# Norm statistics of the first unit by halves of 256 positions, and a new order of the first stage

## The chip, the core and the metric

The kernel runs on one core of one Trainium2 chip. The metric is the device time of one execution in microseconds (us). Five engines of the core work side by side, each through its own list of instructions in order: TensorE (PE in the profile, with PEld for its weight loads), VectorE (DVE), ScalarE (ACT), GpSimd (POOL) and SyncE (SP, which here only issues DMAs). An instruction waits on semaphores until its inputs are there; whatever is listed behind it on the same engine waits with it.

## The reference

One layer: a norm with modulation, an input projection into four parts, a Fourier branch and a recurrent branch with gates, an output projection, a residual and a last norm. What matters here is the head of it:

```python
def rmsnorm(x, g):
    xf = x.astype(jnp.float32)
    y = xf * lax.rsqrt(jnp.mean(xf * xf, axis=-1, keepdims=True) + EPS)
    return (y * g.astype(jnp.float32)).astype(x.dtype)

def modulate(x, g, shift, scale):
    return rmsnorm(x, g) * (1.0 + scale) + shift
...
mod = jax.nn.silu(c) @ w_ada[l] + b_ada[l]
shift, scale, gate = jnp.split(mod[:, None, :], 3, axis=-1)
hx = modulate(x, norm_gain[l], shift, scale)          # x: (1, 2048, 1024)
uf_x, gf_x, ul_x, gl_x = in_proj(hx, w_in[l])         # hx @ w_in, split in four parts of 512
yl_x, _, _ = lru_branch(ul_x, ...)
yf_x = fourier_branch(uf_x, w_four[l])
x = x + gate * out_proj(yf_x, gf_x, yl_x, gl_x, w_out[l])
return rmsnorm(x, final_gain)
```

## The kernel before

The 2048 positions are worked in four units of 512, and the 256 context positions are a fifth. In the first stage a unit's x lies transposed in SBUF: 128 of the 1024 features on the partitions (a k-tile, eight of them), 512 positions along the free dimension. The tiles `xt` hold two k-tiles each. Three multiplications per k-tile and unit go to TensorE:

- `pul` (`mms_ul`, L328): the normalised slice times the weights of the recurrent branch, twelve matmuls of 512 columns; each product is made of three, with operands split in a high and a low part (`hl` and `wu`).
- `ptt` (`mms_tt`, L343): sums and differences of the slice (`f`, split into `eo`) times weights of the Fourier branch (`wf`), twelve matmuls of 260 or 252 columns.
- In the first unit alone also the making of those operands: `part` (`ada_part`, L128) and `o` (`ada_sum`, L143) compute shift and scale of the k-tile from `blk` blocks of w_ada, which `ada_fin` turns into `sh` and `gn`; `pw` (`four_mm`, L168) makes the Fourier weights from `wr`, a slice of w_in.

The first unit has to have its norm statistics before any of this. Its squares `sq` (`square0`, L199) are summed over k-tiles on VectorE (`sum0`, L207); `col0` (L211) sums over partitions by a matmul with ones, four matmuls (eight passes in the profile, since a float32 product takes two) into `ss`; `stats` (L225) takes the root on ScalarE and the reciprocal on VectorE; `spread` (L248) turns that into `pr`, a row per position on all partitions; `prep_x` (L272) multiplies x by it, `prep_hi` (L279) applies `gn` and `sh` and writes the high part of `hl`, `prep_lo` (L312) the low part. Warm-up matmuls (`warm`, L460) on a tile of ones stand ahead.

The order is a list written out by hand, `S1` (L43). Each word is a letter for one of the functions above (`ops`, L477) and its numbers; the program issues them in that order, and each engine gets its own share of them in it. `X` loads x, `a` a half of a w_ada block, `w` a slice of w_in, `0` and `9` small constants; `1`, `+`, `3` are squares, sums and column sums, `T` the root and reciprocal, `P` the spread; `A b c d` make shift and scale, `i j J` the Fourier weights, `u U` the weights of the recurrent branch; `x h l` normalise and split a k-tile, `f e o` fold it; `m` is `pul`, `t` is `ptt`, `!` warm-up, `r` a copy of `pr` into SBUF (`rb`). `x0.1` is unit 0, k-tile 1.

All loads named here are issued by SP in that order on one hardware queue, and `vecs`, a table of small vectors, by ScalarE's queue at the start. SP issues a DMA only when the eighth DMA before it on these queues has landed.

For k-tile 0 `pul` has an order of its own, so that it can begin with the high parts:

```python
if u == 0 and k == 0:
    for s, t in ((0, 0), (1, 0), (0, 1)):
        for c in range(c0, c1):
            nc.tensor.matmul(pul[u][c], w[:, s, P * c:P * c + P], hl[:, t], start=s + t == 0, stop=False)
    return
```

Of the kernel before, what the change touches and what calls it, by code (L numbers as in the profile page):

```python
# [55 lines left out]
def tile_layer(ctx, tc, xp, xnat, xt_in, ctxn, ctxt, w_ada, vec, bgate, fgain, w_in, w_g, w_four, w_gate, w_out,  # L56
# [13 lines left out]
    def r(ap):  # L70
        return ap.bitcast(F32)
# [200 lines left out]
    def prep_x(u, k):  # L272
        n = 256 if u == "c" else 512
        x = xts[u, k // 2][:, k % 2, 0:n]
        nc.vector.tensor_tensor(out=x, in0=x, in1=rb[u][:, 0:n], op=ALU.mult)
# [3 lines left out]
    def prep_hi(u, k):  # L279
        which = 1 if u == "c" else 0  # L280
        n = 256 if u == "c" else 512
        x = xts[u, k // 2][:, k % 2, 0:n]
        h = hs[u, k] = p1.tile([P, 512], F32, name=f"h{u}_{k}", tag="h", bufs=4)
        hl = slab[u, k] = p1.tile([P, 2, 512], F32R, name=f"hl{u}_{k}", tag="hl", bufs=4)
        g, b = gn[:, k, which:which + 1], sh[:, k, which:which + 1]
        if u == 0 and k == 0:
# [1038 lines left out]
```

## Time and profile before

| | us |
|---|---|
| median of 3 runs (653.13 to 653.5) | 653.2 |
| profiled execution, its own time | 653.59 |
| span of its instructions | 651.8 |
| TensorE busy in the span | 642.2 |
| VectorE busy | 524.7 |
| ScalarE busy | 423.9 |
| first `pul` matmul starts at | 16.47 |
| first `ptt` matmul starts at | 22.00 |

Times inside the execution count from the start of the span. In the rows further down a timeline row reads: start, duration, engine, line, operation, out<-in, shapes, count, and in brackets how long the engine had been idle and what released it. TensorE's durations overlap, since matmuls are pipelined: the distance from one start to the next tells what a matmul costs, and the chain of waits shows these distances summed. A granted clock of 1.00 is the upper of TensorE's two levels, 2.4 GHz; the other is 1.2 GHz.

### The profile page before, as it was taken

To read this page: it belongs to the slowest core of one execution; us is meant where nothing else is said; L and a number is where in the kernel's file an instruction comes from. 1 tells how busy PE (TensorE), PEld (TensorE's weight loads), DVE (VectorE), ACT (ScalarE), POOL (GpSimd) and SP (SyncE) were. 2 spreads that over 40 slices of the span, in tenths; PEclk is the share of its full clock that TensorE was granted. 3 is DMA by queue.
4 is the path that set the end of the run, shared out by engine and by line. 5 is a ranking of instruction groups with operands and counts; after the bars stand their busy time and mean duration, and the time that the engine had idled before them with its cause. 6 is when DMAs were issued, how large, how long until landed. Compare 5 with 4: busy or idle time off the path is not lost.

```text
span 651.8 us, 10756 instructions
## 1 busy us (share of the span) xinstructions
PE 642.2 (99%) x4076; PEld 564.9 (87%) x4076; DVE 524.7 (80%) x853; ACT 423.9 (65%) x612; POOL 105.7 (16%) x170
## 2 busy tenths in 40 slices
PE   8999999999999999999999999999999999999996
PEld 8788888888988889899998999999988888888885
DVE  4767999877767668578989898897989697998886
ACT  5575777557554455669597695977844667753752
POOL 0100101023031123442221212212210000000000
PEclk9999999999999999999999999999999999999999
DMA  8996886629597694535443434432477887327533
GB/s 332 417 381 231 244 286 171 246 82 279 151 310 255 236 324 132 166 106 165 129 153 110 145 108 165 123 122 81 145 251 231 290 278 263 107 98 247 184 117 130
DMA packets 69886, 130.22 MB, mean 200 GB/s; under 512 B 7076, under 2 KB 39972, under 8 KB 69834
## 3 DMA queue, kind: packets, MB, share of 16 engines
q1 hardware_dynamic: 51066, 82.36, 39.3%
q0 software_dynamic: 12384, 39.00, 17.8%
q10 hardware_dynamic: 6384, 8.18, 4.0%
q8 instruction: 32, 0.52, 0.3%
q14 instruction: 20, 0.16, 0.1%
HBM read 91.24 MB, written 38.27 MB: 199 GB/s over the span
## 4 chain that ended last, share of the span: by engine, by line
PE 91%; DVE 4%; DMA 2%; issue 2%; ACT 1%; POOL 0%; DVEq 0%; ACTq 0%; POOLq 0%
PE pg L74 9%; PE pg L76 9%; PE pg L75 9%; PE po L75 9%; PE po L76 9%; PE po L74 9%; PE pul L74 5%; PE pul L76 4%; PE pul L75 4%; PE ptt L74 2%; PE ptt L75 2%; PE ptt L76 2%; PE pl L74 2%; PE pl L75 2%; PE pl L76 2%
## 5 line engine op out<-in xcount | busy, mean ns | idle before, releaser
L74 PE MATMUL pg<-hg,wg 128*128 128x256 f32 x512 | 144.1, 282 | 0.1
L75 PE MATMUL pg<-hg,wg 128*128 128x256 f32 x512 | 143.6, 280 | 0.4 <-DVE hg L711 0.4
L76 PE MATMUL pg<-hg,wg 128*128 128x256 f32 x512 | 143.8, 281 | 0.0
L74 PEld LDWEIGHTS pg<-hg,wg 128*128 128x128 f32 x512 | 96.3, 188 | 2.9 <-issue 1.3
L75 PEld LDWEIGHTS pg<-hg,wg 128*128 128x128 f32 x512 | 96.3, 188 | 1.4 <-DVE hg L711 0.7
L76 PEld LDWEIGHTS pg<-hg,wg 128*128 128x128 f32 x512 | 96.4, 188 | 0.0
L427 POOL DMA_DIRECT2D g_d<-gs x80 | 57.8, 724 | 151.9 <-DVE gs L761 72.6
L75 PE MATMUL po<-wo,y 128*128 128x512 f32 x160 | 63.1, 394 | 0.0
L76 PE MATMUL po<-wo,y 128*128 128x512 f32 x160 | 63.1, 394 | 0.0
L74 PE MATMUL po<-wo,y 128*128 128x512 f32 x160 | 62.9, 393 | 0.0
L74 PE MATMUL pul<-hl,wu 128*128 128x512 f32 x124 | 49.9, 402 | 0.0
L76 PE MATMUL pul<-hl,wu 128*128 128x512 f32 x124 | 48.9, 395 | 0.0
L75 PE MATMUL pul<-hl,wu 128*128 128x512 f32 x124 | 48.8, 394 | 0.0
L855 ACT ACTIVATE g<-pl,vecs 128x1024 f32<-128x1024 f32 x32 | 35.4, 1117 | 13.5 <-PE pl L76 13.5
L290 ACT ACTIVATE h<-xt,sh,gn 128x512 f32<-128x512 f32 x31 | 25.2, 813 | 20.4 <-DVE gn L152 10.4
L811 DVE SCALAR_TENSOR_TENSOR v<-up,vecs,v 128x1284 f32<-128x1284 f32 (+1 forms) x24 | 34.1, 1419 | 3.9 <-ACT v L804 3.2
L74 PE MATMUL ptt<-wf,eo 128*128 128x260 f32 (+1 forms) x128 | 36.5, 285 | 0.0
L74 PEld LDWEIGHTS po<-wo,y 128*128 128x128 f32 x160 | 30.3, 189 | 7.1
L76 PE MATMUL ptt<-wf,eo 128*128 128x260 f32 (+1 forms) x128 | 36.2, 283 | 0.0
L75 PE MATMUL ptt<-wf,eo 128*128 128x260 f32 (+1 forms) x128 | 36.2, 283 | 0.0
L76 PEld LDWEIGHTS po<-wo,y 128*128 128x128 f32 x160 | 30.0, 188 | 7.0
L75 PEld LDWEIGHTS po<-wo,y 128*128 128x128 f32 x160 | 30.0, 188 | 6.9
(330 smaller groups left out, 1669.2 us busy)
## 6 DMA issues: line engine op xcount, KB each, us to landing
xt<-in_xt_dram SPq DMA_DIRECT2D x16, 512.0 KB, 5.7
blk<-in_w_ada_dram SPq DMA_DIRECT2D x16, 512.0 KB, 9.4
hr<-h_d SPq DMA_DIRECT2D x32, 256.0 KB, 4.2
xr<-in_xnat_dram SPq DMA_DIRECT2D x16, 512.0 KB, 3.8
g<-g_d SPq DMA_DIRECT2D x15, 512.0 KB, 7.2
out_dram<-xr POOLq DMA_DIRECT2D x14, 512.0 KB, 3.3
dm<-in_dct_dram POOLq DMA_DIRECT2D x12, 514.0 KB, 8.5
x<-in_xp_dram SPq DMA_DIRECT2D x12, 512.0 KB, 5.7
```

Of the source, the lines that this page charges most:

```text
L74: nc.tensor.matmul(out_, lh, rh, start=first, stop=False, skip_group_check=skip)
L75: nc.tensor.matmul(out_, lh, rl, start=False, stop=False, skip_group_check=skip)
L76: nc.tensor.matmul(out_, ll, rh, start=False, stop=last, skip_group_check=skip)
L290: nc.scalar.activation(out=h[:, 0:n], in_=x, func=AF.Identity, scale=g, bias=b)
L427: queue.dma_start(dst[:, :, row:row + s1 - s0], s[:, :, P * i - off + s0:P * i - off + s1])
L811: nc.vector.scalar_tensor_tensor(out=v[:, 0:w], in0=up[:, j:j + w], scalar=cw[:, j:j + 1], in1=v[:, 0:w], op0=ALU.mult, op1=ALU.add)
L855: nc.scalar.activation(out=t[:, c0:c0 + cn], in_=pg[:, 0:cn], func=AF.Sigmoid, bias=vecs[:, q:q + 1])
```

## The change

The statistics of the first unit are made in two halves of 256 positions. Its x comes in another layout, so that a load (`X0.q.hf`) brings one half of the positions of two k-tiles, 256 KB in place of 512 KB; there are eight such loads in place of four, and the second four stand behind the first w_ada block, the first slice of w_in and the small constants. A square now covers two k-tiles of one half (eight squares, all on ScalarE; before seven there and one on VectorE). Of each four squares three are summed on VectorE, so there are two sums per half; two column sums per half (four in all, before three); root, reciprocal and spread run once per half. For k-tile 0 `x`, `h`, `l` and `pul` run by halves: 24 matmuls of 256 columns in place of 12 of 512. All other k-tiles and units are computed as before, in part from strided views of the same tiles.

`S1` is written anew. Its head, up to the first Fourier group `t0.0`, and the diff of the functions:

```diff
-S1 = "X0.0 X0.1 X0.2 X0.3 9 a0.0 a0.1 w0 0 70 !21 10 11 +1 12 13 +2 +3 2 14 15 +5 16 17 4 +7 w1 30 a1.0 a1.1 a2.0 !1 31 !1 32 A0 T0 P0 b0 x0.0 c0 d0 u0 h0.0 U0 a2.1 l0.0 f0.0 i0 e0.0 s0.0 r o0.0 j0 w2 m0.0.0 i1 j1 J0 a3.0 J1 A1 u1 b1 4 w3 m0.0.2 U1 c1 d1 x0.1 h0.1 f0.1 e0.1 t0.0
+S1 = "X0.0.0 X0.1.0 X0.2.0 X0.3.0 9 a0.0 a0.1 w0 0 X0.0.1 2 X0.1.1 X0.2.1 X0.3.1 70 !15 10 11 +1 12 +2 30 13 w1 31 A0 4 a1.0 T0.0 a1.1 a2.0 P0.0 b0 !1 u0 x0.0.0 c0 d0 h0.0.0 U0 l0.0.0 14 15 +5 i0 j0 16 +6 m0.0.0.0 m0.0.2.0 17 32 33 T0.1 P0.1 J0 x0.0.1 A1 b1 h0.0.1 l0.0.1 w2 i1 m0.0.0.1 m0.0.2.1 j1 a3.0 J1 u1 f0.0 e0.0 s0.0 r o0.0 w3 4 U1 a2.1 c1 d1 x0.1 h0.1 f0.1 e0.1 t0.0
...
     def square0(k):
-        x = xts[0, k // 2][:, k % 2, :]
...
-        if k == 7:
-            nc.vector.tensor_tensor(out=sq, in0=x, in1=x, op=ALU.mult)
-        else:
-            nc.scalar.activation(out=sq, in_=x, func=AF.Square)
+        x = xts[0, k % 4][:, k // 4, :]
...
+        nc.scalar.activation(out=sq, in_=x, func=AF.Square)
     def sum0(k):
-        acc = sts["sq", 0 if k < 4 else k - 1]
+        acc = sts["sq", 4 * (k // 4)]
...
     def col0(j):
...
-        acc = sts["sq", (0, 4, 6)[j]]
+        acc = sts["sq", (0, 3, 4, 7)[j]]
         for i in range(4):
-            nc.tensor.matmul(sts["ss"][:, 64 * i:64 * i + 64], acc[:, P * i:P * i + P], ones[:, 0:64],
-                             start=j + i == 0, stop=j == 2, skip_group_check=True)
+            c0 = 128 * (j // 2) + 64 * (i % 2)
+            nc.tensor.matmul(sts["ss"][:, c0:c0 + 64], acc[:, P * i:P * i + P], ones[:, 0:64],
+                             start=j + i == 0, stop=j == 3, skip_group_check=True)
...
-    def stats(u):
+    def stats(u, hf=0):
...
+            nc.scalar.activation(out=st[:, 4 + 2 * hf:6 + 2 * hf], in_=sts["ss"][:, 128 * hf:128 * hf + 128:64],
+                                 func=AF.Sqrt, scale=1.0 / D, bias=eps_t)
+            nc.vector.reciprocal(out=st[:, 2 * hf:2 * hf + 2], in_=st[:, 4 + 2 * hf:6 + 2 * hf])
...
-    def mms_ul(u, k, c0=0, c1=4):
+    def mms_ul(u, k, c0=0, c1=4, hf=None):
...
-        if u == 0 and k == 0:
+        if hf is not None:
+            p0 = 256 * hf
             for s, t in ((0, 0), (1, 0), (0, 1)):
                 for c in range(c0, c1):
-                    nc.tensor.matmul(pul[u][c], w[:, s, P * c:P * c + P], hl[:, t], start=s + t == 0, stop=False)
+                    nc.tensor.matmul(pul[u][c][:, p0:p0 + 256], w[:, s, P * c:P * c + P], hl[:, t, p0:p0 + 256],
+                                     start=s + t + hf == 0, stop=False, skip_group_check=True)
```

On TensorE, from the spread to the first Fourier group (`pr` is the spread, `o_0` and `o_1` the shift and scale of k-tiles 0 and 1, `pw` the Fourier weights, `part` the blocks of w_ada). Before:

```order
L253 MATMUL pr_226<-ident,st_223 128x128 x4
L146 MATMUL o_0_234<-cst,psb_231 128x2
...
L172 MATMUL pw_251<-rmi,wr_143 128x128 x3
...
L337 MATMUL pul_0_266<-hl_0_241,wu_107 128x512
...
L172 MATMUL pw_276<-rmi,wr_191 128x128 x3
...
L134 MATMUL part_287<-blk_0_198,sc_pad 32x256 x4
...
L337 MATMUL pul_2_268<-hl_0_241,wu_107 128x512
...
L146 MATMUL o_1_309<-cst,psb_297 128x2
...
L74 MATMUL ptt_0_324<-wf_115,eo_0_257 128x260
```

On TensorE after the change, the same stretch:

```order
L266 MATMUL pr_207<-ident,st_200 128x128 x2
L477 MATMUL warm<-ones 128x128
L146 MATMUL o_0_215<-cst,psb_210 128x2
...
L172 MATMUL pw_231<-rmi,wr_143 128x128 x3
...
L351 MATMUL pul_0_241<-hl_0_221,wu_107 128x256
...
L351 MATMUL pul_3_244<-hl_0_221,wu_107 128x256
L229 MATMUL ss<-ones,sq_226 128x64 x4
L229 MATMUL ss<-ones,sq_257 128x64 x4
L266 MATMUL pr_207<-ident,st_200 128x128 x2
L134 MATMUL part_273<-blk_0_198,sc_pad 32x256 x4
...
L172 MATMUL pw_289<-rmi,wr_182 128x128 x3
...
L351 MATMUL pul_0_241<-hl_0_221,wu_107 128x256
```

Two column sums and half of the spread now stand behind the first `pul` matmuls, and `part` and `pw` of k-tile 1 and the second half of `pul` stand behind these.

On ScalarE, from the first table load to the first copy of `eo` (`sc_pad` is SiLU of the conditioning out of `vecs`, `sq` the squares, `st` the root, `wu` and `wf` high parts of weights). Before:

```order
L205 ACTIVATE sq_168<-xt_0_129 128x512
...
L479 ACTIVATE sc_pad<-vecs 128x8x2
...
L205 ACTIVATE sq_185<-xt_3_135 128x512
L480 ACT_TABLE_LOAD
L480 ACTIVATE eps_r<-eps_t 128x1
L229 ACTIVATE st_223<-ss,eps_t 128x4
L162 CAST wu_107<-wr_143 128x512
L287 ACTIVATE hl_0_241<-xt_0_129,sh,gn 128x512
L307 CAST eo_0_257<-f_0_248 128x512
```

On ScalarE after the change:

```order
L494 ACTIVATE sc_pad<-vecs 128x8x2
L217 ACTIVATE sq_167<-xt_0_129 128x512
...
L242 ACTIVATE st_200<-ss,eps_t 128x2
L162 CAST wu_107<-wr_143 128x512
L300 ACTIVATE hl_0_221<-xt_0_129,sh,gn 128x256
L217 ACTIVATE sq_226<-xt_0_129 128x512
L217 ACTIVATE sq_228<-xt_1_131 128x512
L176 CAST wf_115<-pw_231 128x512
L217 ACTIVATE sq_238<-xt_2_133 128x512
L217 ACTIVATE sq_257<-xt_3_135 128x512
L242 ACTIVATE st_200<-ss,eps_t 128x2
L300 ACTIVATE hl_0_221<-xt_0_129,sh,gn 128x256
```

SiLU moved ahead of the squares, and the second half's four squares stand behind the first half's `hl`, with one copy of Fourier weights among them.

On TensorE, `part` and `o` of k-tile 4 of the first unit, beside `pul` and `ptt` of k-tile 3. Before:

```order
L134 MATMUL part_492<-blk_0_338,sc_pad 32x256 x4
L134 MATMUL part_492<-blk_1_413,sc_pad 32x256 x4
L74 MATMUL pul_2_268<-hl_3_455,wu_110 128x512
...
L76 MATMUL pul_1_267<-hl_3_455,wu_110 128x512
L146 MATMUL o_4_528<-cst,psb_501 128x2
L147 MATMUL o_4_528<-cst,psb_501 128x2
L74 MATMUL ptt_0_324<-wf_118,eo_3_463 128x260
```

On TensorE after the change, the same place:

```order
L134 MATMUL part_513<-blk_0_357,sc_pad 32x256 x4
L134 MATMUL part_513<-blk_1_419,sc_pad 32x256 x4
L146 MATMUL o_4_533<-cst,psb_522 128x2
L147 MATMUL o_4_533<-cst,psb_522 128x2
L74 MATMUL pul_2_243<-hl_3_473,wu_110 128x512
...
L76 MATMUL pul_1_242<-hl_3_473,wu_110 128x512
L74 MATMUL ptt_0_342<-wf_118,eo_3_481 128x260
```

`o_4`, which reads VectorE's copy `psb` of `part`, moved from behind the twelve `pul` matmuls to right behind `part`. Behind this k-tile a few pairs of instructions change places on ScalarE, VectorE and SP; POOL's list is the same.

## Rows read from the trace of the kernel before

**Rows 1.** The page: busy time of TensorE in the span.
```profile
PE 642.2 (99%) x4076; PEld 564.9 (87%) x4076; DVE 524.7 (80%) x853; ACT 423.9 (65%) x612; POOL 105.7 (16%) x170
```

**Rows 2.** Waits of TensorE, 0 to 90 us: total, times, longest.
```profile
PE warm L462 <- DVE eps_t L85: 1.1, 1, 1.1
PE ss L216 <- DVE sq L209: 0.8, 1, 0.8
PE pul L337 <- ACT hl L287: 0.4, 1, 0.4
```

**Rows 3.** Timeline of the first 17 us, statistics to the first `pul`.
```profile
5.43 2.54 ACT L205 ACTIVATE sq<-xt 128x512 f32<-128x512 f32 x4 [2.74 <-DMA xt<-in_xt_dram]
5.61 0.17 DVE L445 TENSOR_SCALAR b<-vecs 128x8 f32<-128x8 f32 x1 [4.25 <-DMA vecs<-in_vec_dram]
7.87 0.20 ACT L479 ACTIVATE sc_pad<-vecs 128x16 f32<-128x16 f32 x1
9.30 0.63 ACT L205 ACTIVATE sq<-xt 128x512 f32<-128x512 f32 x1 [0.15 <-DMA xt<-in_xt_dram]
9.95 1.28 ACT L480 ACT_TABLE_LOAD   x1
12.47 0.26 ACT L229 ACTIVATE st<-ss,eps_t 128x4 f32<-128x4 f32 x1 [1.02 <-PE ss L216]
12.77 0.18 DVE L232 RECIPROCAL st<-st 128x4 f32<-128x4 f32 x1 [1.49 <-ACT st L229]
13.56 0.62 ACT L162 CAST wu<-wr 128x512 fp32r<-128x512 f32 x1 [0.82 <-DMA wr<-in_w_in_dram]
15.30 0.27 DVE L152 TENSOR_SCALAR gn<-o,b,vecs 128x2 f32<-128x2 f32 x1
16.47 1.67 PE L337 MATMUL pul<-hl,wu 128*128 128x512 f32 x6 [0.43 <-ACT hl L287]
```

**Rows 4.** Chain of waits: start, what TensorE's groups cost.
```profile
11.45 0.98 PE ss L216 x8
13.44 1.10 PE pr L253 x8
18.14 1.06 PE pw L172 x10
19.20 1.00 PE part L134 x16
```

**Rows 5.** Operations of 256 columns (the context unit): min/median/max ns.
```profile
L275 DVE TENSOR_TENSOR xtc<-xtc,rbc x8: 418/420/423, 167.1 to 180.8; 128x256 f32<-128x256 f32 x8
L290 ACT ACTIVATE hc<-xtc,sh,gn x8: 598/602/612, 168.2 to 181.8; 128x256 f32<-128x256 f32 x8
```

**Rows 6.** Timeline, 17 to 24 us: the first Fourier group and its operands.
```profile
18.06 0.62 ACT L307 CAST eo<-f 128x512 fp32r<-128x512 f32 x1 [1.64 <-DVE f L300]
18.71 0.69 DVE L319 TENSOR_TENSOR eo<-f,eo 128x512 fp32r<-128x512 f32 x1 [0.68 <-ACT eo L307]
22.00 0.37 PE L74 MATMUL ptt<-wf,eo 128*128 128x260 f32 x1
23.52 0.72 PE L172 MATMUL pw<-rmi,wr 128*128 128x128 f32 x5
```

**Rows 7.** Timeline, k-tile 4: VectorE's copy of `part`, which ended at 39.6.
```profile
39.70 0.42 DVE L140 COPY psb<-part 128x256 f32<-128x256 f32 x1 [1.78 <-PE part L134]
```

**Rows 8.** By stretch: busy of PE, PEld, DVE, ACT, POOL; granted clock; DMA share; GB/s.
```profile
10.00:16.47 6.47, 6.04 (x60) 5.18 (x59) 3.65 (x9) 3.13 (x5) 0.01 (x1) 1.00 1.03 415
```

**Rows 9.** By stretch, warm-up matmuls alone: TensorE's busy time and passes, weight loads, clock.
```profile
3.00:5.40 2.40, 2.40 (x13) 2.40 (x13) 1.00 0.93 351
5.50:7.90 2.40, 2.40 (x23) 2.40 (x22) 1.00 1.03 405
```

**Rows 10.** By stretch at the tail: no TensorE work after 645.5.
```profile
648.00:650.00 2.00, 0.00 (x0) 0.00 (x0) 0.00 (x0) 0.13 (x1) 0.00 (x0) 1.00 0.93 351
650.00:652.00 2.00, 0.00 (x0) 0.00 (x0) 0.00 (x0) 0.00 (x0) 0.00 (x0) 0.65 0.08 28
```

More of the change, by code (lines that the diff above doesn't have):

```diff
@@ L182, in tile_layer, with load_xt, x_of, pos_of @@
     rb, xts = {}, {}
-    def load_xt(u, q):
+    def load_xt(u, q, hf=None):
         n = 256 if u == "c" else 512
-        t = p1.tile([P, 2, 512], F32, name=f"xt{u}_{q}", tag="xt", bufs=XB)
-        nc.sync.dma_start(t[:, :, 0:n], ctxt[:, 2 * q:2 * q + 2, :] if u == "c" else xt_in[u, :, 2 * q:2 * q + 2, :])
-        xts[u, q] = t
+        if not hf:
+            xts[u, q] = p1.tile([P, 2, 512], F32, name=f"xt{u}_{q}", tag="xt", bufs=XB)
+        t = xts[u, q]
+        if u == 0:
+            nc.sync.dma_start(t[:, hf, :], xt_in[u, :, 2 * q + hf, :])
+        else:
+            nc.sync.dma_start(t[:, :, 0:n], ctxt[:, 2 * q:2 * q + 2, :] if u == "c" else xt_in[u, :, 2 * q:2 * q + 2, :])
+    def x_of(u, k, hf=None):
+        if u:
+            return xts[u, k // 2][:, k % 2, 0:256 if u == "c" else 512]
+        x = xts[0, k // 2][:, :, 256 * (k % 2):256 * (k % 2) + 256]
+        return x if hf is None else x[:, hf, :]
+    def pos_of(u, ap, hf=None):
+        if u:
+            return ap[:, 0:256 if u == "c" else 512]
+        return ap.rearrange("p (a j) -> p a j", a=2) if hf is None else ap[:, 256 * hf:256 * hf + 256]
     xns = {}
@@ L246, in stats, with spread @@
         sts[u] = dgs
-    def spread(u):
+    def spread(u, hf=0):
         n = 2 if u == "c" else 4
-        pr = ps1.tile([P, 512], F32, name=f"pr{u}", tag="tr")
+        pr = rb[0] if hf else ps1.tile([P, 512], F32, name=f"pr{u}", tag="tr")
         if u == 0:
-            for i in range(4):
+            for i in range(2 * hf, 2 * hf + 2):
                 nc.tensor.matmul(pr[:, P * i:P * i + P], sts[0][:, i:i + 1].to_broadcast([P, P]), ident, start=True, stop=True)
@@ L270, in tile_layer, with prep_x, prep_hi @@
     slab = {}
[L272 to L275, printed above, removed]
+    def prep_x(u, k, hf=None):
+        x = x_of(u, k, hf)
+        nc.vector.tensor_tensor(out=x, in0=x, in1=pos_of(u, rb[u], hf), op=ALU.mult)
     hs, fs, eos = {}, {}, {}
-    def prep_hi(u, k):
+    def prep_hi(u, k, hf=None):
         which = 1 if u == "c" else 0
[L281 to L284, printed above, removed]
+        x = x_of(u, k, hf)
+        if not hf:
+            hs[u, k] = p1.tile([P, 512], F32, name=f"h{u}_{k}", tag="h", bufs=4)
+            slab[u, k] = p1.tile([P, 2, 512], F32R, name=f"hl{u}_{k}", tag="hl", bufs=4)
+        h, hl = pos_of(u, hs[u, k], hf), pos_of(u, slab[u, k][:, 0, :], hf)
         g, b = gn[:, k, which:which + 1], sh[:, k, which:which + 1]
-        if u == 0 and k == 0:
-            nc.scalar.activation(out=hl[:, 0], in_=x, func=AF.Identity, scale=g, bias=b)
+        if hf is not None:
+            nc.scalar.activation(out=hl, in_=x, func=AF.Identity, scale=g, bias=b)
             nc.vector.tensor_scalar(out=h, in0=x, scalar1=g, scalar2=b, op0=ALU.mult, op1=ALU.add)
         else:
-            nc.scalar.activation(out=h[:, 0:n], in_=x, func=AF.Identity, scale=g, bias=b)
-            nc.scalar.copy(hl[:, 0, 0:n], h[:, 0:n])
+            nc.scalar.activation(out=h, in_=x, func=AF.Identity, scale=g, bias=b)
+            nc.scalar.copy(hl, h)
     def fold_x(u, k):
```

31 lines of the change are left out of this document (15 added, 16 removed).

## The prediction

> **What bounds the kernel now.** The page comes first: TensorE is busy for 642.2 of 651.8 us [rows 1], so time is gained or lost where TensorE stands still or does what another order would spare. Its waits come next: in the first 90 us it has three, and the last is 0.4 us before the first `pul` [rows 2]. From 16.47 on it works without a pause, the Fourier group of k-tile 0 included (22.00 to 23.52) [rows 3, 6]. So two numbers decide: when the first `pul` starts, and how much TensorE waits behind it. Whatever it is late by at 23.52 it carries to the end, since nothing later waits in that kernel for anything but TensorE's own results. Why `pul` starts only at 16.47 is read from the timeline: squares from 5.43 on as x comes, the last x at 9.30, the root at 12.47, the reciprocal at 12.77, `gn` until 15.57 [rows 3]. By stretch DMA is full there (share 1.03, 415 GB/s) [rows 8].
>
> **Part 1: how much earlier `pul` starts.** I follow the new lists with the old durations, each engine in its order, a consumer some 0.06 us behind its producer.
> SiLU of `vecs` now stands ahead of the squares. `vecs` is there at 5.61, its SiLU costs 0.20 [rows 3]; the first x, half the bytes, will be there by then. So four squares, 2.54 us [rows 3], run from 5.8 to 8.35. The third is done at 7.7; behind it VectorE's second sum (0.69, the price of a 512-column operation of two operands [rows 6]) ends at 8.6. Two column sums of 0.98 [rows 4] take TensorE to 10.6. The table load of 1.28 [rows 3] lies beside them. Root 0.26 and reciprocal 0.18 [rows 3] end at 11.15, under `part` (1.00 [rows 4]), which ends at 11.6: its blocks now have 1 MB less ahead of them, 2.5 us at 415 GB/s, so they are no later than that. Half a spread (half of 1.10 [rows 4]) ends at 12.15, `prep_x` of 256 columns (0.42 [rows 5]) at 12.6. `o_0` runs from 12.4 to 12.8, and shift and scale, 0.4 (0.27 for `gn` [rows 3], and what `sh` is ahead of it), end at 13.35. The high part of 256 columns is 0.60 on ScalarE [rows 5], so halving it saves little. `wu` is ready, as its load (13.56 before [rows 3]) also has 1 MB less ahead of it. First `pul`: 14.05 in place of 16.47, **2.4 us earlier**.
>
> **Part 2: work that moves behind it.** Two column sums (2 x 0.95; before, all three stood ahead) and half a spread (0.5) [rows 4] now stand between the first `pul` and the Fourier group: **+2.4**. There is one column sum more than before, and it is in that number. The 24 half matmuls cost what the 12 whole ones do: twelve of 260 or 252 columns take 1.52 [rows 6], or 0.127 each, against 1.67 for six of 512 with their tail [rows 3]. I put **-0.1** for that. With parts 1 and 2 alone the change is worth nothing.
>
> **Part 3: new waits of TensorE.**
> Between the first `pul` pieces VectorE's low parts (`wu`, `hl`) arrive just late: 0.2 (an estimate; 0 to 0.7, one whole VectorE operation [rows 6]).
> *Second squares.* x of the second half has as many bytes ahead of it as `wr` and `rmi` had before; `wr` was there at 13.56 [rows 3], so it comes by about 13.8, as ScalarE ends the first `hl` (14.0). There follow two squares (1.27), a copy of Fourier weights (0.58, a little under the 0.62 of a cast [rows 6]) and the third square (0.64): 16.45, and the sum 0.69: 17.2. TensorE is through with the twelve half matmuls at 14.05 + 12 x 0.12 + 0.2 = 15.7 and the next in its list is the column sum. `part` and `pw` of k-tile 1, ready to run, are queued behind it. Wait **1.55**.
> *Second root.* Column sums end at 19.15; root and reciprocal (0.26 + 0.18 and three handovers) hold the spread: **0.65**. Before, both were passed once, ahead of everything.
> *Operands of the Fourier group.* The spread ends at 20.3, `part` at 21.3, `pw` (1.06 [rows 4], 1.16 with its start) at 22.45, the second half of `pul` at 23.95, `o_1` at 24.3. But `f` is queued on VectorE behind the low part of `pw`'s copy: copy until 23.2, low part until 23.9, `f` as two of 0.42 until 24.7, `eo` on ScalarE 0.62 until 25.4 [rows 6]: wait **1.1**; its low part, 0.69 [rows 6], holds the third matmul until 26.1: **0.5**. Before, `eo` was ready at 19.4 and the group began at 22.00 [rows 6].
> *k-tile 1.* VectorE comes out of this about as late as TensorE and the next low part is awaited too: I take **0.3** (0, if it catches up, to 0.6, one of its operations).
> *`o_4` right behind `part`.* VectorE's copy starts 0.1 behind `part` and takes 0.42 [rows 7]; with the handover and the first weight load TensorE stands **0.7**. Before, twelve matmuls lay between, and the copy cost nothing.
> Sum of the waits: 0.2 + 1.55 + 0.65 + 1.1 + 0.5 + 0.3 + 0.7 = 5.0.
>
> **Sum.** -2.4 + 2.4 - 0.1 + 5.0 = **+4.9**. The profiled execution took 653.59 about its span of 651.8; with 4.9 it is 658.5. The median of the runs shown is 0.4 lower, so the forecast is **658.1 us**.
>
> Other edits cost nothing: an eighth square on ScalarE is already counted in the 2.54; later swaps of pairs are covered by TensorE's queue of `pul` matmuls, which starts nothing late today [rows 2]; if that cover were gone, each would cost at most one operation, 0.69 [rows 6]. VectorE's strided views have the same element counts, and I take the same time (bounds: no gain; 0.69 more, a whole operation, which on k-tiles 2 to 7 lies beside TensorE).
>
> **A page on loads.** Four more loads are issued by SP, between `rmi` and the next `wr`. The DMA share of 1.03 at 415 GB/s with loads of 512 KB [rows 8] shows that whatever each load costs by itself is hidden in the queue; the same bytes go in the same place, so I put 0. The Trainium skill, page "DMA: Bandwidth & Descriptors", section "Bandwidth", says to batch transfers to 1 MiB or more, since each has some 2 us of fixed cost. By that rule four more loads would put the second half's x some 8 us later and the sum near +10 (an estimate from that page); the trace speaks against it.
>
> **The rivals.**
> *The head start is kept (faster).* If `vecs` and the first x land 1.6 us sooner, `pul` starts at 12.45, where `wu`'s own load bounds it (13.56 less 2.5, plus the cast 0.62, and `hl` behind). For it: a smaller load ahead, a queue of its own. It pays only where the second statistics are ready whenever TensorE comes to them, so that all of part 3 goes: -4.0 + 2.4 - 0.1 = -1.7, **651.5**. It decides from the point at which the second squares need not wait for the first `hl`; ScalarE's list has them behind it.
> *The waits are hidden, nothing changes.* TensorE would have to reach the second column sum at 17.2 or later with all else as estimated, or the operands come sooner: parts 1 and 2 alone, **653.1**. Against it: its list has nothing else to run there.
> *The clock falls.* TensorE now pauses from about 6.6 (fifteen warm-up calls in place of 21) to 8.6, and again at 15.7, 19.1 and 24.3. At the start the passes run at the lower level: 13 touch 2.40 us and later 23 the same stretch [rows 9]; the record begins later and shows 1.00 there. At the tail TensorE had been idle since 645.5, and the clock was still 1.00 in 648 to 650 and 0.65 on average in the next stretch [rows 10]; so pauses of 2 us have not been seen to bring it down. If it fell once and stayed as long as at the start (1.05 to 5.4), 4.35 us at 13/23 of the pace lose 1.9: **660.0**. The Trainium skill, page "TensorE: Matmul & The Clock Gate", section "HAM oscillation — how this bites in real kernels", warns that idle gaps between bursts of matmuls bring the clock back to half; by that rule the pauses here would be a reason to expect this case, and the tail of this trace bounds it.
> *`vecs` sooner, the rest as forecast.* The first x instead of `vecs` sets the squares; at most 0.96 of part 1 (the last of four halves would bound them): 657.1. I count this in the forecast's range.
>
> **How the numbers follow.** Forecast 0.80, its own range 656.4 (0.96 from `vecs`, 0.7 from part 3's small waits) to 659.4 (low parts at 0.7, k-tile 1 at 0.6, 0.5 for handovers). Clock 0.09, nothing changed 0.06, faster 0.05. The range reaches a little beyond the forecast's on both sides, 655.4 to 660.4, and takes in the clock's case. About 0.2%, 1.3 us, can be told from no change: faster 0.05, same 0.06, slower 0.89.
>
> **What would show it.** The first `pul` at 14.0 (part 1); a gap of 1.5 between it and the third column sum, and root, reciprocal and spread in a row with TensorE idle (part 3); first Fourier matmul near 25.4 and the group's end near 27.4 in place of 23.52; 0.7 idle ahead of `o_4`; no further waits, so that the span's end moves as the end of the first unit does. I am wrong if the first Fourier group ends by 24, or if TensorE later stands still less than before.

## The result and the profile after

| | before | after |
|---|---|---|
| median, 5 executions each (us) | 653.5 (653.13 to 654.46) | 658.36 (657.85 to 660.78) |
| ratio, 95% interval | | 1.007, 1.0046 to 1.0094 |
| profiled execution, and its span | 653.59, 651.8 | 657.85, 656.1 |
| first `pul` / first `ptt` / end of its group | 16.47 / 22.00 / 23.52 | 13.61 / 24.62 / 26.64 |
| `pw` of k-tile 7 starts at | 58.18 | 62.00 |

The change costs 4.9 us by the medians and 4.3 in the profiled execution. The executions of after spread over 3 us, and their mean granted clock goes with it: 0.996 to 0.998 for the three at 657.85 to 658.36, 0.994 for 659.96 and 0.990 for 660.78. So beside medians I give the median of the executions with a clock of 0.996 or more: 658.05 for after (three executions), and 653.91 for before (63 executions, run beside the experiments below; 5 more had a lower clock). Executions over 1.5% above the fastest of the same kernel are in no median or ratio: one of e_order (696.87, clock 0.85), one of e_comb (1053.66, 0.56) and three of e_gap (669.41 to 675.95, 0.97 to 0.98).

The page, busy time of the engines after; it answers to [rows 1].

```profile
PE 642.1 (98%) x4082; PEld 564.5 (86%) x4082; DVE 524.3 (80%) x855; ACT 425.3 (65%) x615; POOL 105.5 (16%) x170
```

TensorE does as much as before (642.2) in a span that is 4.3 longer: all of the loss is standing still. Its waits, 0 to 95 us, answer to [rows 2] (total, times, longest):

```profile
PE ss L229 <- DVE sq L221: 1.5, 2, 0.8
PE warm L477 <- DVE eps_t L85: 1.1, 1, 1.1
PE part L134 <- DMA blk<-in_w_ada_dram: 1.0, 1, 1.0
PE ptt L74 <- ACT eo L320: 0.9, 1, 0.9
PE pr L266 <- DVE st L244: 0.6, 1, 0.6
PE o L146 <- DVE psb L140: 0.5, 1, 0.5
PE ptt L76 <- DVE eo L332: 0.2, 1, 0.2
```

Before had 0.8 ahead of the column sums and 0.4 ahead of `pul`; after has six kinds of waits, all but one of them new. The timeline of the head, answering to [rows 3] and [rows 6]:

```profile
4.21 0.22 ACT L494 ACTIVATE sc_pad<-vecs 128x16 f32<-128x16 f32 x1 [1.53 <-DMA vecs<-in_vec_dram]
4.33 2.35 ACT L217 ACTIVATE sq<-xt 128x512 f32<-128x512 f32 x4
10.63 0.64 PE L134 MATMUL part<-blk,sc_pad 128*32 128x256 f32 x8 [1.01 <-DMA blk<-in_w_ada_dram]
11.94 0.62 ACT L162 CAST wu<-wr 128x512 fp32r<-128x512 f32 x1 [2.59 <-DMA wr<-in_w_in_dram]
12.65 0.27 DVE L152 TENSOR_SCALAR gn<-o,b,vecs 128x2 f32<-128x2 f32 x1
13.61 1.96 PE L351 MATMUL pul<-hl,wu 128*128 128x256 f32 x12
14.97 1.15 ACT L217 ACTIVATE sq<-xt 128x512 f32<-128x512 f32 x2
16.38 2.00 PE L229 MATMUL ss<-ones,sq 128*128 128x64 f32 x16 [0.81 <-DVE sq L221]
18.93 0.71 PE L266 MATMUL pr<-ident,st 128*128 128x128 f32 x4 [0.55 <-DVE st L244]
22.56 0.69 DVE L180 TENSOR_TENSOR wf<-pw,wf 128x512 fp32r<-128x512 f32 x1 [0.57 <-ACT wf L176]
23.95 0.62 ACT L320 CAST eo<-f 128x512 fp32r<-128x512 f32 x1 [0.91 <-DVE f L313]
24.62 0.39 PE L74 MATMUL ptt<-wf,eo 128*128 128x260 f32 x1 [0.90 <-ACT eo L320]
26.64 1.22 PE L172 MATMUL pw<-rmi,wr 128*128 128x128 f32 x10
43.37 0.38 PE L146 MATMUL o<-cst,psb 128*128 128x2 f32 x2 [0.55 <-DVE psb L140]
```

`pw` of k-tile 7, before and after:

```profile
58.18 1.22 PE L172 MATMUL pw<-rmi,wr 128*128 128x128 f32 x10
62.00 1.22 PE L172 MATMUL pw<-rmi,wr 128*128 128x128 f32 x10
```

`pul` starts 2.86 us sooner, and the lateness shows from the column sums of the second half on: the Fourier group ends 3.1 late, `pw` of k-tile 7 starts 3.8 late (`o_4` is the last row of the timeline). The clock stood at 1.00 in this execution as long as TensorE had work. Behind 95 us TensorE waited 1.8, for `yf` and `hg`, against 0.7 before. In the thirteen traces other than e_gap's, the rest of the span from `pw` of k-tile 7 on took 592.7 to 594.9 us whatever had been edited ahead of it (before 593.6, after 594.1), so half a microsecond there can't be told from scatter.

### The profile page after: what moved, and what is told of

The parts are those of the page before. It is cut to its first block, busy times and chain, and to the rows that moved or that the text cites. A ratio compares the mean times of both kernels' runs of the same rounds, so it can differ in the third digit from the quotient of the medians.

```text
span 656.1 us, 10785 instructions
## 1 busy us (share of the span) xinstructions
PE 642.1 (98%) x4082; PEld 564.5 (86%) x4082; DVE 524.3 (80%) x855; ACT 425.3 (65%) x615; POOL 105.5 (16%) x170
## 3 DMA queue, kind: packets, MB, share of 16 engines
q0 software_dynamic: 12384, 39.00, 17.7%
## 4 chain that ended last, share of the span: by engine, by line
PE 85%; DMA 5%; issue 5%; DVE 4%; ACT 1%; POOL 1%; DVEq 0%; POOLq 0%; ACTq 0%
PE pg L74 9%; PE pg L76 9%; PE pg L75 9%; PE po L75 9%; PE po L76 9%; PE po L74 8%; PE pul L74 5%; PE pul L76 4%; PE pul L75 4%; PE ptt L76 2%; PE ptt L74 2%; PE ptt L75 2%; DMA ul_d<-usc 2%; PE pl L74 2%; PE pl L75 2%
```

## The experiments

Four theories were at stake. A: TensorE lacks work while the second half's statistics and operands are made, and each pause counts by itself. B: a chain (loads, or statistics to operands) is the bound, and the pauses only mirror it. C: the halves themselves cost (smaller loads, more instructions). D: the pauses bring TensorE's clock down. "At full clock" stands for executions with a mean clock of 0.996 or more; ratios are to before, as it ran beside the same group of experiments. There were three groups (the first four rows of the table, the next four, the last four), in which before had 653.6, 653.75 and 654.0 at full clock; after ran in none of them. So a difference of under 0.4 us between groups, or between after and an experiment, can't be told from none.

| | median (n) | ratio, 95% | at full clock (n) | `pw` of k-tile 7 |
|---|---|---|---|---|
| e_o4 | 657.57 (6) | 1.0047 to 1.0077 | 657.2 (4) | 61.41 |
| e_fill | 657.64 (6) | 1.0051 to 1.0075 | 657.6 (5) | 61.97 |
| e_order | 656.56 (11) | 1.0008 to 1.0051 | 654.6 (6) | 59.05 |
| e_warm | 657.25 (5) | 1.0045 to 1.0069 | 657.3 (5) | 62.49 |
| e_f0 | 657.17 (6) | 1.0027 to 1.0054 | 657.1 (5) | 62.29 |
| e_nostat2 | 657.35 (12) | 1.0032 to 1.0078 | 657.2 (8) | 62.20 |
| e_load8 | 656.02 (12) | 1.0020 to 1.0047 | 655.0 (7) | 61.25 |
| e_half0 | 654.44 (12) | 0.9988 to 1.0036 | 654.4 (11) | 57.81 |
| e_gap | 663.35 (3) | 1.0084 to 1.0153 | none | 60.70 |
| e_delay | 655.22 (12) | 1.0005 to 1.0039 | 655.1 (10) | 59.98 |
| e_pk2 | 655.98 (5) | 1.0019 to 1.0043 | 655.8 (4) | 59.28 |
| e_comb | 655.82 (9) | 1.0019 to 1.0039 | 655.8 (8) | 61.12 |

**e_order: the halves in the old order.**

```diff
-X0.0.0 X0.1.0 X0.2.0 X0.3.0 9 a0.0 a0.1 w0 0 X0.0.1 2 X0.1.1 X0.2.1 X0.3.1 70 !15 10 11 +1 12 +2 30 13 w1 31 A0 4
+X0.0.0 X0.1.0 X0.2.0 X0.3.0 X0.0.1 X0.1.1 X0.2.1 X0.3.1 9 a0.0 a0.1 w0 0 2 70 !21 10 11 +1 12 +2 13 14 15 +5 16 +6 17 4 w1 30 31 a1.0 a1.1 a2.0 !1 32 33 A0
...
```

> The functions, the half loads, the half statistics (four column sums) and the half matmuls of the changed kernel, but the order of before: all eight x loads first, both halves' statistics together ahead of the first pul, o_4 at its old place. Theory (the order costs, the halves do not): first pul near 16.3 without pauses behind it over 0.5 in all, 653.5 to 654.3, as before. Rival (halves cost by themselves: smaller packets, one column sum more, 24 matmuls in place of 12): 655.5 to 658. Rival (clock): 653.5 too, and a spread as small as before's.

First `pul` at 16.72, group end at 24.41, at full clock 654.6, between what the theory and the rival had. So the new order costs some 3.4 of the 4.1 us (658.05 to 654.6), the halves with their loads 0.7 (1.0 against before in the same group). TensorE's waits in this kernel, 0 to 95 us:

```profile
PE warm L477 <- DVE eps_t L85: 1.1, 1, 1.1
PE pul L351 <- ACT hl L300: 0.3, 1, 0.3
PE pul L351 <- DVE wu L166: 0.2, 1, 0.2
PE ss L229 <- DVE sq L221: 0.2, 1, 0.2
```

**e_o4: one pause taken away.** `c4` back behind `m0.3.0`.

> Only the two matmuls of o_4 go back to their old place behind the pul matmuls of k-tile 3; all else is the changed kernel. Theory (TensorE runs out of work in the first unit, and every pause is lost for good): the pause of 0.6 to 0.7 us ahead of o_4 goes, pw of k-tile 5 starts at 47.4 in place of 48.14, time 657.7 against 658.4. Rival (the pause is a symptom, the next operand is late by as much): pw of k-tile 5 stays at 48.1 and the time at 658.4. Rival (the clock falls in some runs): 658.4, same spread of 3 us.

`pw` of k-tile 5 started at 47.55 in place of 48.14, as theory A has it: 0.6 in the first unit by the trace, 0.85 by the medians at full clock. The traced execution itself, at 657.89, was no faster than after's 657.85: the rest behind the first unit took 0.6 longer in it.

**e_fill: the pause filled with `pw`.**

```diff
-17 32 33 T0.1 P0.1 J0 x0.0.1 A1 b1 h0.0.1 l0.0.1 w2 i1 m0.0.0.1 m0.0.2.1 j1 a3.0 J1
+17 i1 j1 J1 32 33 T0.1 P0.1 J0 x0.0.1 A1 b1 h0.0.1 l0.0.1 w2 m0.0.0.1 m0.0.2.1 a3.0
```

> pw of k-tile 1, its copy and its low part move ahead of the third column sum, into the pause of 0.8 us there; all else is the changed kernel. Theory (TensorE lacks work while the second statistics are made, and VectorE's low part of pw is what holds up f): third column sum 0.35 later (16.7), but 1.16 us of pw less between part and the second half of pul, and f no longer behind the low part: the first Fourier group ends near 25.4 in place of 26.64, time 657.1. Rival (the chain x, squares, sums, root, spread, operands is the bound, and TensorE's pauses only mirror it): the later third column sum makes everything behind it 0.35 later, 658.7. Rival (clock): no change beyond the spread.

The group ended at 26.62, as without the edit (26.64): theory A failed here, and the trace goes with B, though nothing became later either. TensorE in this kernel:

```profile
16.49 1.33 PE L172 MATMUL pw<-rmi,wr 128*128 128x128 f32 x10 [0.76 <-DMA wr<-in_w_in_dram]
17.65 1.95 PE L229 MATMUL ss<-ones,sq 128*128 128x64 f32 x16
23.26 1.22 PE L351 MATMUL pul<-hl,wu 128*128 128x256 f32 x8 [0.51 <-DVE hl L328]
```

`pw` stood in the same pause, waiting for its own load. The column sum then came 1.3 later, and what `pw` gave back further on, the later statistics took. Of the work next in TensorE's list nothing was loaded that could have filled the pause.

**e_nostat2: no second statistics.** `14 15 +5 16 +6 17 32 33 T0.1` left out.

> The changed kernel without the second half's statistics: its four squares, two sums, two column sums, root and reciprocal are left out, and the first half's reciprocals stand in for them. This takes 1.93 us of TensorE and pauses of 0.81 and 0.55 us from in front of the second half spread. Theory (loads bound this stage: behind the statistics the next thing late is the load of w for k-tile 1, at 16.5, and the second block of w_ada for part of k-tile 1, at 18 to 19): part of k-tile 1 starts at 17.8 to 18.3, not at 16.3, the second half of pul at 20.0 to 20.5 in place of 21.71, 656.7. Rival (the second statistics alone are the loss): all 3.3 us come back, second half of pul at 18.4, 655.0. Rival (the pauses do no harm): only the 1.93 of column sums come back.

```profile
15.52 0.61 PE L266 MATMUL pr<-ident,st 128*128 128x128 f32 x4
17.66 0.64 PE L134 MATMUL part<-blk,sc_pad 128*32 128x256 f32 x8 [1.53 <-DMA blk<-in_w_ada_dram]
18.80 0.96 PE L134 MATMUL part<-blk,sc_pad 128*32 128x256 f32 x8 [0.50 <-DMA blk<-in_w_ada_dram]
19.68 2.40 PE L172 MATMUL pw<-rmi,wr 128*128 128x128 f32 x10
```

The spread came 3.4 sooner, and `part` of k-tile 1 then stood for its two loads until 17.66 and 18.80, as theory B's loads had it. How much of the 3.3 comes back this execution can't say: the clock fell right behind these waits (`pw` took 2.16 in place of 1.14). At full clock the gain was 0.9, nearer to the 1.6 that the loads leave than to 3.3: taking the second statistics away gives back less than they cost, since the loads are awaited next.

**e_f0: the fold first.** `f0.0 e0.0 o0.0` ahead of `j1`.

> The changed kernel with the fold of k-tile 0 and its two casts (f, eo, eo low) ahead of the copy and the low part of k-tile 1's pw on ScalarE and VectorE. Theory (the chain from the second statistics to eo bounds the first Fourier group): f follows the low part of hl at 22.0, eo is there at 23.4, TensorE starts the group right behind o_1 at 23.6 in place of 24.62, its first third waits 0.4 for eo's low part, and the group ends at 25.7 to 26.0 in place of 26.64. What is then later: pw's copy and low part of k-tile 1 and wu's, so that 0.2 to 0.6 comes back at the pul of k-tile 1; pw of k-tile 2 at 33.2 in place of 33.66, 657.6 to 658.0. Rival (what the group lacks is another operand, as wf's low part): end at 26.6, 658.4. Rival (clock): no change beyond the spread.

In the traced execution the group started at 24.53 and ended at 26.47, though the clock had dropped under it (by stretch: busy of PE, PEld, DVE, ACT, POOL; granted clock; DMA share; GB/s):

```profile
18.00:20.00 2.00, 1.50 (x8) 1.13 (x12) 0.99 (x3) 0.25 (x1) 0.00 (x0) 0.53 1.01 408
20.00:22.00 2.00, 2.00 (x20) 0.88 (x13) 0.53 (x3) 0.60 (x1) 0.00 (x0) 0.62 1.03 422
22.00:24.00 2.00, 2.00 (x20) 2.00 (x19) 1.50 (x5) 0.36 (x1) 0.60 (x1) 1.00 1.02 414
```

The spread and `part` took 3.02 there where after has 1.64, and the wait for `eo` was gone. Of the executions at full clock the median is 657.1, 0.9 less than after. e_comb, further down, has the same edit, and its trace is at full clock; its Fourier group ended 0.7 sooner than after's, though its first `pul` started 0.4 later:

```profile
25.93 1.22 PE L172 MATMUL pw<-rmi,wr 128*128 128x128 f32 x10
```

So the chain from the second statistics to `eo` held the group, and 0.7 to 0.9 of it was the order of VectorE's list.

**e_load8 and e_pk2: what the halved loads cost.** Both are the kernel before; e_load8 has eight x loads of 256 KB, e_pk2 four of 512 KB whose packets are 2 KB.

```diff
-nc.sync.dma_start(t[:, :, 0:n], ... xt_in[u, :, 2 * q:2 * q + 2, :])
+for i in range(2): nc.sync.dma_start(t[:, i, :], xt_in[u, :, 2 * q + i, :])   # e_load8
+nc.sync.dma_start(t[:, :, 0:n], ... xt_in[u, :, q:8:4, :])                      # e_pk2
```

> The kernel before, with one edit: each 512 KB load of the first unit's x is two of 256 KB, one for each k-tile, in the same place of the queue; nothing else moves. Theory (halved loads move their bytes more slowly: 314 GB/s between the fourth and the eighth of them where 405 stood with whole loads): the last x lands 0.6 later, at 9.9, the column sums end at 13.0, w of k-tile 0 lands near 14.2 in place of 13.56, first pul 16.9 to 17.1 in place of 16.47, 654.0 to 654.2 against 653.5. Rival (the same bytes go in the same time, what my prediction took): first pul at 16.47, 653.5. Rival (some 2 us for each load of its own): x lands 8 us later, first pul near 24.

> The kernel before with its four x loads of 512 KB, each now k-tiles q and q+4 in place of 2q and 2q+1, so that a load's packets are 2 KB in place of 4 KB while the number of loads stays at four; the code reads each k-tile from its new place. It tells what made eight loads of 256 KB slower. If it is the packets (84 ns for 2 KB against 159 for 4 KB, 6% more for each byte): last column sum 0.3 to 0.5 later than 11.33, w of k-tile 0 at 13.9, 653.9 to 654.5. If it is the number of loads: all as before, last column sum at 11.33, 653.5 to 653.9.

The last column sum began at 11.87 in e_load8 and at 12.45 in e_pk2, against 11.33 (10.84 and 10.87 in e_half0 and e_delay, whose x loads are those of before); the first `pul` of e_pk2 at 17.59 against 16.47. (In e_load8's traced execution the clock fell, so its `pul` at 19.53 tells nothing of the loads.) At full clock e_load8 took 1.3 and e_pk2 1.8 more than before in their groups, and e_pk2's 1.1 on the last column sum is more than the 0.3 to 0.5 expected. So shorter rows, or the stride between them, make the x loads later with four loads too; it doesn't take a larger number of loads. The 2 us for each load that the Trainium skill's page in my prediction gives would have been 8 (an estimate from that page). By stretch, before, then e_pk2 while x comes and right behind it:

```profile
4.00:6.00 2.00, 2.00 (x13) 2.00 (x13) 0.17 (x1) 0.57 (x2) 0.00 (x0) 1.00 1.04 412
6.00:8.00 2.00, 2.00 (x19) 1.92 (x18) 1.28 (x2) 1.87 (x5) 0.00 (x0) 1.00 1.02 403
```

```profile
4.00:6.00 2.00, 2.00 (x11) 2.00 (x11) 0.00 (x0) 0.12 (x1) 0.00 (x0) 1.00 0.96 306
6.00:8.00 2.00, 2.00 (x16) 2.00 (x16) 0.69 (x1) 1.24 (x3) 0.00 (x0) 1.00 0.96 303
10.00:12.00 2.00, 2.00 (x18) 2.00 (x19) 1.59 (x3) 1.77 (x3) 0.00 (x0) 1.00 1.03 416
```

After has a slow stretch too, from 6 to 8 us:

```profile
4.00:6.00 2.00, 2.00 (x17) 2.00 (x17) 0.67 (x2) 1.77 (x4) 0.00 (x0) 1.00 1.08 373
6.00:8.00 2.00, 1.30 (x13) 1.11 (x11) 0.89 (x2) 1.91 (x3) 0.00 (x0) 1.00 1.00 307
10.00:12.00 2.00, 1.37 (x15) 0.96 (x16) 0.48 (x2) 0.06 (x1) 0.00 (x0) 1.00 1.02 369
```

The DMA share reads 0.96 to 1.08 in all of them: busy engines, fewer bytes. But after's slow stretch is not that of its x rows. What moved from 6 to 8 us was this (the view of the DMA queues):

```profile
DMA packets 165, 0.61 MB, mean 307 GB/s; under 512 B 15, under 2 KB 15, under 8 KB 165
```

That is 4 KB a packet: the first w_ada block and `wr`. The x rows of 2 KB ahead of them had moved 377 GB/s from 3 to 5 us. So e_pk2 shows that shorter x rows can cost this much, and not that they are what made the loads of after late; that cause stays open. The Trainium skill, page "DMA: Bandwidth & Descriptors", section "Specifications", has transfers from 512 B on at line rate; in e_pk2 rows of 2 KB were slower than those of 4 KB before by a quarter, and the measurement decides.

**e_gap and e_warm: the clock.** e_gap is before with `!13` for `!21`. e_warm is after with `!18` for `!15`, `!4` ahead of `A0`, and passes in two more pauses.

> The kernel before with 13 warm-up calls in place of 21 ahead of the first column sum; nothing else differs. TensorE then stands still for some 2.5 us there in place of 0.84. Theory (a pause that is long enough brings the clock to its lower level, and this is what the slower executions of the changed kernel and its variants have): the granted clock is 0.50 from about 9 for some 6 us in most executions, the mean clock 0.990 to 0.994 where before has 0.997 and more, and part, the spread and pw behind run at half the pace: 656 to 657.5. Rival (the lower clock comes by chance or from the chip, not from pauses): as before, 653.5 to 653.9, and a lower clock as seldom as before has it. Rival (only work that is delayed counts): 653.5.

> The changed kernel with passes of the warm-up kind (their result is not used) in three pauses of TensorE: three more ahead of the first column sum, four ahead of part of k-tile 0, three ahead of the third column sum, four ahead of the first Fourier group. Theory (waits for data): 658.4 within 0.5, since the pauses are filled with nothing that counts and at most 0.2 us of each is overrun. Rival (the clock falls in some executions because of these pauses): the spread of 657.9 to 660.8 closes to under 1 us and the median falls below 657.9, with a granted clock of 0.998 in every run.

All six executions of e_gap had a low clock (0.970 to 0.994) and took 657.93 to 675.95. TensorE, and the clock by stretch, in the traced one:

```profile
8.41 1.10 PE L216 MATMUL ss<-ones,sq 128*128 128x64 f32 x8 [1.67 <-DVE sq L209]
13.36 1.94 PE L134 MATMUL part<-blk,sc_pad 128*32 128x256 f32 x16
```

```profile
8.00:10.00 2.00, 1.59 (x13) 1.59 (x14) 1.65 (x3) 1.76 (x4) 0.00 (x0) 0.95 1.02 335
10.00:12.00 2.00, 2.00 (x12) 2.00 (x11) 0.69 (x1) 1.01 (x2) 0.00 (x0) 0.50 1.02 416
14.00:16.00 2.00, 2.00 (x17) 0.98 (x8) 0.42 (x1) 0.23 (x1) 0.00 (x0) 0.50 1.03 420
16.00:18.00 2.00, 2.00 (x18) 2.00 (x17) 0.94 (x3) 0.00 (x0) 0.00 (x0) 0.85 1.02 418
```

One pause of 1.67, and the clock stood at 0.50 from about 10 to past 16: `part` took 1.86 in place of 1.00. Theory D's mechanism is shown: a longer pause, and the low clock in six executions of six, where before has it in 5 of 68. The loss was larger than expected (656 to 657.5), since TensorE later waited 4.4 us for `usc` in the traced execution and the clock fell again (0.50 from 192 to 200); what made that wait is not shown. e_load8's traced execution shows the same behind a pause of 1.35. The Trainium skill, page "TensorE: Matmul & The Clock Gate", section "HAM oscillation — how this bites in real kernels", warns of idle gaps between bursts; these runs agree.

The pauses of after bring the clock down in a part of the executions only: the eight kernels with x in 2 KB packets and no extra passes (after among them) had a clock under 0.996 in 21 of 63 executions, e_warm and e_comb in 1 of 14, before in 5 of 68 (counting every execution, 22 of 64 and 2 of 15). That the passes of e_warm and e_comb keep the clock up is likely by these counts, and not more. Why e_order, whose traced execution has no wait over 0.3 behind the start, was among the frequent ones (5 of 11) stays open: none of its executions at a low clock was traced. e_warm's first unit was 0.5 later than after's (62.49), yet its median at full clock is 0.8 less; in its trace the gain lies behind the first unit (592.7 us against 594.1), and what makes it is open. Its executions still spread from 656.4 to 658.6, so not all of the spread is the clock.

**e_half0: halves without new work between.** Before, with the spread, `x`, `h`, `l` and `pul` of k-tile 0 by halves and `o_0` between the halves of the spread.

> The kernel before with whole x loads, whole statistics and its order up to the root, but k-tile 0 spread, normalised and multiplied by halves: half the spread, o_0, the other half; shift and scale right behind the first half's x; the first half of pul as soon as its high part is there; the second behind pw and part of k-tile 1. Theory (halves pay where they shorten a chain that TensorE waits for and put no new work between): gn at 14.9 in place of 15.57, first pul at 16.1 right behind pw of k-tile 0, without the 0.43 us of waiting, and no pause behind it: the group ends at 23.1 in place of 23.52, 653.1. Rival (VectorE's five operations more come too late for the low parts): TensorE waits 0.3 to 0.6 in the pul pieces, 653.5 to 653.8. Rival (halves cost more on TensorE than whole ones): 654.

First `pul` at 15.68, group end at 23.16. But x had landed half a microsecond sooner in this execution (last column sum at 10.84 against 11.33), so the gain in the first `pul` is 0.3 and in the group's end none. 654.4 at full clock: no gain. In this trace TensorE waited behind `part` only 0.2, for `o`, up to the group's end.

**e_delay: is lateness carried?** Before with `!10` ahead of `A0`.

> The kernel before with ten more warm-up calls ahead of part of k-tile 0: 2.1 us of work that counts for nothing, at 0.21 each, and no other edit. Theory (what TensorE is late by in the first unit is carried to the end): first pul at 18.5, pw of k-tile 7 at 60.3 in place of 58.18, and the time 2.1 more, 655.6 to 656.0. Rival (later waits for operands take part of it back): under 655.0. Rival (lateness sets off further waits behind it): over 656.5.

```profile
11.81 2.45 PE L462 MATMUL warm<-ones 128*128 128x128 f32 x20
18.29 1.67 PE L337 MATMUL pul<-hl,wu 128*128 128x512 f32 x6 [0.44 <-ACT hl L287]
```

In the traced execution the passes held `part` up for 2.38 us; x had landed 0.5 sooner, `pw` of k-tile 7 came 1.8 later, and the time was 2.0 more than that of before's profile (655.59 to 653.59). The medians at full clock differ by only 1.2 (1.1 within the group). Theory and rival are both inside the interval; whether some 0.8 is regained in the typical execution stays open.

**e_comb: three edits together.** e_f0's, e_o4's, and e_warm's passes but for those ahead of the Fourier group.

> The changed kernel with three edits together: the fold of k-tile 0 ahead of pw's copy and low part, o_4 at its old place, and warm-up calls (their result is not used) in the pauses ahead of the first column sum, of part of k-tile 0 and of the third column sum. Theory (each pause counts by itself, so the edits add): of 658.1, what the changed kernel's executions at a clock of 0.996 and more have, 0.7 to 0.9 go for each of the first two edits: 656.4, and no execution with a lower clock. It stays slower than before by 2.5, which is the order of the loads and of the statistics. Rival (the edits gain the same microseconds): 657.2. Rival (with them the new order wins): 653.5 or less.

At full clock 655.8, 2.3 less than after, where the single gains add to 0.9 + 0.9 + 0.8. But in the traced execution (655.72) the first unit gained only 0.9 of 2.1 (`pw` of k-tile 7 at 61.12); the rest of the gain lies behind it, where 592.8 us stand against 594.1, inside the scatter. So that the edits add up in the first unit is not shown. It is still slower than before, by 1.8 to 1.9 us. No version was found that beats the kernel before.

## Why the prediction was right, point by point

The time (658.1 forecast, 658.36 measured) and its direction came out, by the mechanism forecast: an early start, and pauses behind it that cost more. The closeness of the number is in part luck. The sum of +4.9 was worked out for the first unit, which came out 3.8 late; 0.5 more came behind it, inside the scatter, and the median of five has two executions at a low clock in it.

- Part 1: 2.4 forecast, 2.86 measured. The squares began at 4.33, not 5.8, as `vecs` was there 1.5 sooner than in [rows 3]. That alone would have been worth more (it is the condition of the rival that keeps the head start, with `pul` at 12.45), but the loads took 0.9 back: I had the first blocks and `wr` earlier by 1 MB at 415 GB/s [rows 8] and priced the halved loads at 0. `wu` could start at 11.94, where 11.05 follows from that working, and `part` stood 1.0 for its second block. This step failed: from 6 to 8 us the DMA engines moved 307 GB/s and not 415. Why is open; e_pk2 shows only that shorter x rows can cost as much (1.1 us on the last column sum).
- Part 2: +2.4 forecast, 2.57 measured: two column sums 1.93, half a spread 0.64.
- Part 3, forecast and measured, by the distances between starts: low parts and second squares 0.2 + 1.55, 0.5 + 0.8; second root 0.65, 0.6; `eo` 1.1, 1.05; its low part 0.5, 0.5 (the group took 2.02 in place of 1.52); k-tile 1 0.3, 0.1; `o_4` 0.7, 0.6. Each wait stood at its place; the longest was mis-sized, at half of what I gave it, as ScalarE came to the second squares at 13.46 and not at 14.0, and these and the copy among them took 0.3 less. In sum 5.0 forecast, 4.2 measured; with -2.86, +2.57 for part 2 and -0.1 that is 3.8, the lateness at `pw` of k-tile 7.
- "Parts 1 and 2 alone are worth nothing" came out nearly: by the trace -2.86 and +2.57 leave 0.3 us. And the halves gain nothing in the old order (e_order, 0.7 to 1.0 slower than before). In each of the stretches shown up to 12 us the DMA share is 0.96 or more, so that, as I read it and no run isolates, another order decides mainly which operand is missing.
- "Wait 1.55: `part` and `pw` of k-tile 1, ready to run, are queued behind it" was wrong. They weren't ready: `wr` of k-tile 1 was there at 16.49 (e_fill), the blocks at 17.7 and 18.8 (e_nostat2).
- The clock rival had 660.0 at a chance of 0.09, and a low clock is there in two executions of five: 659.96 and 660.78. My ground against it, that 2 us without work had not brought the clock down at the tail [rows 10], was wrong: e_gap shows a fall behind 1.67.
- "No further waits" is not borne out by the trace: behind 95 us TensorE waited 1.1 longer than before, though the rest grew by only 0.5. Whether the change makes these waits is open, as the rest scatters from 592.7 to 594.9.

## What to carry to other kernels

Work that waits for a statistic can be started early by halves only if other work, with its operands loaded, stands ready while the second half is made; where the loads are the bound, as in this first stage, the early start turns into pauses behind it, and the second half's chain (squares, sum, root, spread, operands) stands in TensorE's way. Such pauses don't come back one by one: without the second statistics (3.3 us) the median fell by 0.9. Before filling a pause, look up when the load of the filler lands. Splitting a tensor into halves along its contiguous direction can also halve its packets: compare the rate of the loads, not the DMA share.

## What the runs showed of the hardware

- From 4 to 8 us, x loads with rows of 2 KB moved 305 (e_pk2), 309 (e_order) and 331 GB/s (e_load8), where those with rows of 4 KB moved 404 to 407 in four traces (before, e_half0, e_delay, e_gap), at a DMA share of 0.96 to 1.03. It is no fixed rate of such rows: after's moved 377 GB/s from 3 to 5 us, and 4 KB rows behind them 307.
- A pause of 1.35 (e_load8) or 1.67 us (e_gap) was followed by the lower clock, not in the pause but 2.3 and 1.4 us into the work behind it, for some 6.8 us in both. In e_f0 and e_nostat2 it lasted 3.4 us. Behind a pause of 1.20 in e_pk2's traced execution it stayed at 1.00.
- The small load of `vecs`, on a queue of its own, was there at 2.54 to 4.40 in the ten traces with first x loads of 2 KB rows, and at 5.06 to 5.61 in the four with 4 KB rows. It is not the size of the loads: the earliest is e_pk2, whose x loads have 512 KB.

```profile
2.54 0.17 DVE L446 TENSOR_SCALAR b<-vecs 128x8 f32<-128x8 f32 x1 [1.18 <-DMA vecs<-in_vec_dram]
```
